# Scheduling priority for softmax chains, longer leads of fill, and an output pair whose operands load in two parts, in a two-layer hybrid decoder trunk

## The chip, the core and the metric

The kernel runs on one core of a Trainium2 chip. The metric is the device time of one execution in microseconds (us), the median over several runs. The core has a matrix engine (TensorE, "PE" in the profile, with its weight loads as "PEld"), three elementwise engines (VectorE "DVE", ScalarE "ACT", GpSimd "POOL") and SyncE ("SP"), which here issues nearly all DMAs. Each engine works through its own instructions in the order of the program.

## The reference

Two layers over a sequence of 1024 tokens with 1024 features, float32. Each layer adds the mixer's output and then a cross-attention over 256 memory tokens; a last norm follows.

```
for l in range(2):
    h = rms_norm(x, norm_mix_w[l])
    proj = h @ w_in                       # one projection for all three groups
    ya = sliding_window_attention(rope(q_a), rope(k_a), v_a, sinks) * silu(g_a)   # 8 heads, 2 kv heads, window 128
    yb = forgetting_attention(q_b, k_b, v_b, log_sigmoid(f_b + b)) * silu(g_b)    # 8 heads ("FoX"), causal, with decay
    yc = rms_norm((ssd(conv(xbc), dt, a) + d_skip * xs) * silu(z))                # state-space scan, chunks of 128
    x = x + concat(ya, yb, yc) @ w_out
    hq, mem_n = rms_norm(x, norm_xq_w[l]), rms_norm(mem, norm_mem_w[l])
    x = x + softmax((hq @ wq) @ (mem_n @ wk).T / 16) @ (mem_n @ wv) @ wo          # 4 heads of 256
return rms_norm(x, final_norm_w)
```

Both attentions normalise their scores with a softmax.

## The kernel before

Each float32 operand of a matmul is split into a high part and a remainder (`hi` on ScalarE, `lo` on VectorE or GpSimd), and each product is three matmuls (`mm3`, L111 to L113): high x high, low x high, high x low. Weights are streamed from memory and split on the way (`wload`: tiles `wst`, `whi`, `wlo`).

The order of work has two authors. TensorE's order is the order in which the Python code emits its matmuls. That order is made by `weave(main, fill)`: `main` is a generator for a chain with waits in it (a softmax, a norm), `fill` one for independent matmuls (projections, output products). Both yield costs, which add up to an estimated clock, `self.clock`. When `main` yields a number, the fill is advanced by that number times `self.ratio`, through an account called `owed`; when `main` yields a tuple `(time,)`, the fill is advanced until the estimated clock reaches that time, and what it takes is subtracted from `owed`; when `main` yields a string, the fill is advanced until that name is in `self.ready`. A fill that yields `None` has nothing to give for now. A "lead" below is such a wait of a fixed length: `yield (self.clock + 5.0,)`.

The order on the other engines and the DMA queues is made by a planner when the program is built. It keeps a priority for every instruction, the order of emission, and takes the first one that it thinks is ready; inside `tc.high_priority(n)` an instruction counts as if it had been emitted n places earlier.

The stages of one layer, with the lines that matter here:

- `tokmaj`: token-major projections (values, gates of the scan). In the second layer the norm of the second half of the sequence runs as `main` against the value projections of the first half.
- `mixer`: `fox_attend`, then `swa_attend`, then `ssd_scan` as `main`; as `fill` the projections of q, k and gates, the convolution and the output products. A FoX row (`fox_scores`) is scores on TensorE, maximum on VectorE (L604), negation (L605), exponential on ScalarE (L607), reciprocal (L608), normalisation on GpSimd (L609). Two rows are turned by `fox_turn` (transposes at L630, split at L77 and L85) and multiplied with the values at L667. A sliding-window unit (`swa_scores`, `swa_turn`) does the same for two heads at L779 to L791, with transposes at L802 and products at L834; the add at L542 collects the result and frees its PSUM buffer. `at[...]` says from when on a row may be turned. The rotary embedding of the sliding-window queries (`roped`, L720 and L721), gates (`gate`, L509 and L510) and weight splits use the same engines.
- `outproj`: the output product. For the first half of the sequence and the attention groups its first two tiles run as a pair, over the eight operand tiles in the order (4, 5, 6, 7, 0, 1, 2, 3); the last one is computed late and awaited by name (`y30`). The others are reloaded from memory into space of the normed activations (`load_ys`: a DMA, a cast on ScalarE, a subtraction on VectorE or GpSimd). The pair needs both accumulators (`acc`, two buffers), which the gate before it frees through L509 and L510.
- `tail`: the rest of the output product (`out_c`), the cross-attention and its output (`finish`). A norm (`norm_half`) begins with a lead; then `rstd` sums squares over partitions with small matmuls (L221), `spread` computes the inverse root and puts it on a diagonal (L232 to L242), waits through a second lead, and spreads it over all partitions with two matmuls (L251); then every tile is scaled (`normed`, L270) and split.

Of the kernel before, what the change touches and what calls it, by code (L numbers as in the profile page):

```python
# [12 lines left out]
ALU = mybir.AluOpType  # L13
# [30 lines left out]
class Net:  # L44
    def __init__(self, ctx, tc, a, out):
        self.ctx, self.tc, self.nc, self.a, self.out = ctx, tc, tc.nc, a, out
        self.n = 0
        self.pq = None
        self.alt_w = True
        self.ready, self.ratio, self.clock = set(), 1.0, 0.0  # L50
        self.alt = 0
        self.nb, self.ntp = 3, 2

    def psum(self):
        return self.tc.tile_pool(name=self.nm("pq"), bufs=1, reuse_waits="tile", space=PSUM)
# [172 lines left out]
    def spread(self, pool, ps, nch, rr):  # L228
        nc = self.nc
        with self.tc.high_priority(100):  # L230
            ms = self.tile(pool, [P, 4], F32, "nms", 2)
            nc.vector.tensor_scalar(out=ms[:, :nch], in0=ps[:, :nch], scalar1=EPS, scalar2=None, op0=ALU.add)  # L232
            rs = self.tile(pool, [P, 4], F32, "nrs", 2)
            nc.gpsimd.tensor_tensor(out=rs[:, :nch], in0=ms[:, :nch], in1=self.mhalf[:, :nch], op=ALU.pow)

            rp = self.tile(pool, [P, 2, 4], F32R, "nrp", 2)
            nc.vector.tensor_copy(rp[:, 0, :nch], rs[:, :nch])
            self.lo(rp[:, 1, :nch], rs[:, :nch], rp[:, 0, :nch])
            dg = self.tile(pool, [P, 2, 4, P], F32R, "ndg", 1)
            B3 = [P, nch, P]  # L240
            for i in range(2):
                nc.vector.tensor_tensor(  # L242
                    out=dg[:, i, :nch], in0=self.ident[:, None, :].to_broadcast(B3),
                    in1=f(rp[:, i, :nch, None]).to_broadcast(B3), op=ALU.mult,
                )
        self.rs = rs
        yield (self.clock + 5.0,)
        n = nch * P
        pb = self.tp()
        for i in range(2):  # L250
            nc.tensor.matmul(  # L251
                pb[:, :n], self.ones, dg[:, i, :nch].rearrange("p c d -> p (c d)"), start=i == 0, stop=i == 1
            )
        yield 0.43
        nc.scalar.copy(rr, pb[:, :n])
        return rr
# [16 lines left out]
        self.lo(lo, t[:, :n], hi, eng=nc.gpsimd if self.alt else nc.vector)  # L273

    def norm_half(self, pool, xs, accs, w, half):
        yield (self.clock + 3.0,)
        rr = yield from self.rstd(pool, accs, HALF)
        c = slice(half * HALF, (half + 1) * HALF)
        for k in range(KT):
            self.normed(pool, xs[k], w[:, k : k + 1], rr, HALF, self.hhi[:, k, c], self.hlo[:, k, c])  # L280
# [305 lines left out]
    def fox_scores(self, pool, t, e, i):  # L586
        nc = self.nc
        mm = nc.tensor.matmul
        Q1, Q2, K1, K2, _ = self.state["fox", t]
        n = (i + 1) * P  # L590
        S = self.big()
        q = slice(i * P, (i + 1) * P)
        cost = 0.0
        for b in range(0, n, HALF):
            w = min(HALF, max(256, n - b))
            diag = i * P < b + HALF
            k = slice(b, b + w)
            mm(S[:, k], Q1[e][:, q], K1[e][:, k], start=True, stop=False)  # L598
            mm(S[:, k], Q2[e][0:68, q], K2[e][0:68, k], start=False, stop=not diag)  # L599
            if diag:  # L600
                mm(S[:, q], self.identb, self.nmaskb, start=False, stop=True)  # L601
            cost += 2 * w / 2400 + 0.05 * diag
        sm = self.tile(pool, [P, 4], F32, "sm", 4)
        nc.vector.tensor_reduce(out=sm[:, 0:1], in_=S[:, :n], axis=AX.X, op=ALU.max)  # L604
        nc.vector.tensor_scalar(out=sm[:, 1:2], in0=sm[:, 0:1], scalar1=-1.0, scalar2=None, op0=ALU.mult)  # L605
        Pt = self.tile(pool, [P, T], F32, "Pt", 4)
        nc.scalar.activation(Pt[:, :n], S[:, :n], AF.Exp, bias=sm[:, 1:2], scale=1.0, accum_out=sm[:, 2:3])  # L607
        nc.vector.reciprocal(sm[:, 3:4], sm[:, 2:3])  # L608
        nc.gpsimd.tensor_scalar(  # L609
            out=Pt[:, :n], in0=Pt[:, :n], scalar1=sm[:, 3:4], scalar2=1.0, op0=ALU.mult, op1=ALU.mult  # L610
        )
        return Pt, cost


    def fox_turn(self, pool, Ps, kb, last):
# [9 lines left out]
        for d in range(2):  # L625
            for s in range(2):
# [1 line left out]
                    continue  # L628
                o = (2 * (1 - d) + s) * P
                nc.tensor.transpose(pt[:, o : o + P], Ps[s][:, (kb + d) * P : (kb + d + 1) * P], self.ident)  # L630
        self.hi(ph[:, c0:], pt[:, c0:])
        self.lo(pl[:, c0:], pt[:, c0:], ph[:, c0:])
        return ph, pl

    def fox_attend(self, l, pool):
# [5 lines left out]
        def scores(r):  # L641
            if r < len(rows):
                t, e, i = rows[r]
                if e == i == 0:
                    yield f"fox{t}"
                probs[r], cost = self.fox_scores(pool, t, e, i)
                yield cost
                at[r] = self.clock + 2.5 + 0.45 * (i + 1)

        at = {}  # L650
        yield from scores(0)
# [109 lines left out]
    def swa_scores(self, pool, t, i):  # L761
# [12 lines left out]
        for e in range(2):  # L774
            o = S[:, e * 256 : (e + 1) * 256]
            mm(o, Q1[e][:, q], K1[:, k0 : k0 + 256], start=True, stop=False)
            mm(o, Q2[e][:, q], K1[:, k0 : k0 + 256], start=False, stop=True)
        for e in range(2):
            nc.vector.tensor_tensor_reduce(  # L779
                out=Pt[:, e, :256], in0=S[:, e * 256 : (e + 1) * 256], in1=self.band[:, min(i, 1), :], scale=1.0,  # L780
                scalar=-3e38, op0=ALU.add, op1=ALU.max, accum_out=mx[:, 0, e : e + 1],
            )

        nc.vector.scalar_tensor_tensor(mx[:, 1], mx[:, 0], -1.0, self.nsk[:, h0 : h0 + 2], ALU.mult, ALU.min)
        for e in range(2):
            nc.scalar.activation(
                Pt[:, e, :257], Pt[:, e, :257], AF.Exp, bias=mx[:, 1, e : e + 1], scale=1.0, accum_out=mx[:, 2, e : e + 1]
            )
        nc.vector.reciprocal(mx[:, 3], mx[:, 2])
        o = Pt[:, :, :256]  # L790
        nc.gpsimd.tensor_tensor(out=o, in0=o, in1=mx[:, 3, :, None].to_broadcast([P, 2, 256]), op=ALU.mult)  # L791
        return Pt

    def swa_turn(self, pool, Pt):
# [73 lines left out]
    def mixer(self, l):  # L868
# [16 lines left out]
        def fill():  # L885
# [16 lines left out]
            for t in range(4):  # L902
# [4 lines left out]
                yield from self.noted(f"swag{t}", self.gate(l, t, T_GA + t, (0, 1) if t < 3 else (1, 0)))  # L907

            ys = self.early_ys
            self.load_ys(ys, order[:-1], 0)  # L910
            yield from self.noted(
                "ab0", self.outproj(self.fp, ("th", 3), l, 0, 0, ys, order, xin, pair=True, last="y30")
            )
            while "ab" not in self.ready:
                yield None
# [368 lines left out]
                put(values, pc, c, ps)  # L1284


    def outproj(self, pool, tag, l, half, s, ys, order, xin, after=None, pair=False, last=None):
        a = self.a
        c = slice(half * HALF, (half + 1) * HALF)
        for ms in ((0, 1), 2, 3, 4, 5, 6, 7) if pair else range(KT):  # L1290
            ms = ms if pair and ms == (0, 1) else (ms,)
            xt, ws, ps = {}, {}, {}
            for m in ms:
# [2 lines left out]
                ws[m] = self.wload(a["w_out"][l, m, s])  # L1296
                ps[m] = self.acc()
            for i, k in enumerate(order):
                while last and i == KT - 1 and last not in self.ready:
                    yield None  # L1300
                for m in ms:
# [25 lines left out]
    def tail(self, l, fp):  # L1327
# [9 lines left out]
        with self.pool("ma", 2) as ma:  # L1337
# [125 lines left out]
            self.weave(attend(1), finish(0, range(KT)))  # L1463
            self.ratio = 0.0
            if not last:
                self.weave(self.norm_half(pool, *self.sums[0], wn, 0), finish(1, range(KT)))
                return tl, (), self.norm_half(pool, *self.sums[1], wn, 1)
            self.weave(close(0, slice(0, HALF)), finish(1, range(KT - 1)))

# [153 lines left out]
```

## Time and profile before

| | |
|---|---|
| median of 3 runs | 2539.09 us (2537.62 to 2541.44) |
| the profiled execution | 2551.32 us, span of its instructions 2549.3 us |
| mean granted TensorE clock in it | 0.984 |
| TensorE busy | 2466.7 us |
| VectorE, ScalarE, GpSimd busy | 1545.4, 1189.0, 1166.9 us |
| memory read, written | 238.72 MB, 86.81 MB |

The profile is of one execution. Its views: the page with busy times; a table of stretches of time, with the busy time of each engine and the clock granted to TensorE (1.00 is full speed); the waits (which operation of an engine stood idle for which other one: total, times, longest); and the timeline, instruction by instruction (start, length, engine, line, operation, output<-inputs, and in brackets the idle time before it and what ended it). In the timeline a matmul's start-to-start distance tells more than its length, since matmuls overlap.

### The profile page before, as it was taken

How to read it: one execution, taken by the hardware profiler on the slowest of the kernel's cores; microseconds unless marked ns; L12 is line 12 of the kernel's file. 1: busy time of each engine (PE TensorE's matmuls, PEld its weight loads, DVE VectorE, ACT ScalarE, POOL GpSimd, SP SyncE). 2: the span in 40 equal slices, each digit the busy share in tenths (PEclk: the TensorE clock that was granted, in tenths of full speed). 3: DMA queues.
4: the chain of work that ended last, by engine and by line, in shares of the span. 5: the costliest groups of instructions: out<-in, count | busy, mean ns of one | idle time of the engine just before them, and what ended most of it. 6: DMA issues, size and time to landing. Idle time of an engine off the chain costs nothing.

```text
span 2549.3 us, 39348 instructions
## 1 busy us (share of the span) xinstructions
PE 2466.7 (97%) x13900; PEld 2081.7 (82%) x13900; DVE 1545.4 (61%) x2716; ACT 1189.0 (47%) x2455; POOL 1166.9 (46%) x1193
## 2 busy tenths in 40 slices
PE   8799999999999999999999999999999999999997
PEld 7799988888788777888879988888877877787886
DVE  6923166666778688654464226666668868764355
ACT  5532155545556455434443225455546645543442
POOL 5732144435566487432252124444446657732233
PEclk9999999999999999999999999999999999999999
DMA  7774132222222766553464223222223376554333
GB/s 235 217 237 111 65 98 70 66 88 86 81 87 90 246 221 195 162 169 116 128 195 120 78 68 92 70 79 84 89 71 90 115 256 209 170 185 151 119 93 132
DMA packets 230360, 333.37 MB, mean 131 GB/s; under 512 B 24370, under 2 KB 107442, under 8 KB 230148
## 3 DMA queue, kind: packets, MB, share of 16 engines
q1 hardware_dynamic: 228292, 328.76, 41.4%
q8 instruction: 110, 1.80, 0.3%
q10 hardware_dynamic: 1872, 2.10, 0.2%
q14 instruction: 86, 0.70, 0.1%
HBM read 238.72 MB, written 86.81 MB: 128 GB/s over the span
## 4 chain that ended last, share of the span: by engine, by line
PE 78%; DVE 7%; DMA 5%; issue 3%; ACT 3%; POOL 3%; SPq 1%; DVEq 0%; POOLq 0%; ACTq 0%
PE acc L111 16%; PE acc L112 15%; PE acc L113 15%; PE tp L667 3%; PE tp L630 2%; PE acc L372 2%; PE big L372 2%; PE acc L374 2%; PE big L374 2%; PE acc L373 2%; PE big L373 2%; SPq L72 1%; PE big L598 1%; PE big L599 1%; PE s L1128 1%
## 5 line engine op out<-in xcount | busy, mean ns | idle before, releaser
L111 PE MATMUL acc<-hhi,whi 128*128 128x512 f32 (+1 forms) x1960 | 796.8, 407 | 6.8 <-DVE th L510 5.4
L113 PE MATMUL acc<-hlo,whi 128*128 128x512 f32 (+1 forms) x1960 | 772.0, 394 | 0.0
L112 PE MATMUL acc<-hhi,wlo 128*128 128x512 f32 (+1 forms) x1960 | 771.6, 394 | 0.0
L85 POOL TENSOR_TENSOR wlo<-wst,whi 128x512 fp32r<-128x512 f32 x279 | 377.5, 1353 | 337.5 <-ACT whi L77 280.7
L113 PEld LDWEIGHTS acc<-hlo,whi 128*128 128x128 f32 x1960 | 372.0, 190 | 82.2
L111 PEld LDWEIGHTS acc<-hhi,whi 128*128 128x128 f32 x1960 | 374.2, 191 | 67.3 <-DVE th L510 5.8
L112 PEld LDWEIGHTS acc<-hhi,wlo 128*128 128x128 f32 x1960 | 373.8, 191 | 57.7
L77 ACT CAST whi<-wst 128x512 fp32r<-128x512 f32 x420 | 259.5, 618 | 302.8 <-PE acc L113 206.0
L77 ACT CAST ph<-tp 128x512 fp32r<-128x512 f32 (+1 forms) x256 | 142.5, 556 | 168.8 <-PE tp L630 118.0
L85 DVE TENSOR_TENSOR pl<-tp,ph 128x512 fp32r<-128x512 f32 (+1 forms) x256 | 167.0, 652 | 78.3 <-ACT ph L77 76.3
L85 DVE TENSOR_TENSOR wlo<-wst,whi 128x512 fp32r<-128x512 f32 x141 | 128.4, 910 | 118.0 <-ACT whi L77 117.2
L609 POOL TENSOR_SCALAR Pt<-Pt,sm 128x128 f32<-128x128 f32 (+7 forms) x128 | 105.8, 827 | 182.6 <-DVE sm L608 180.0
L1015 DVE SCALAR_TENSOR_TENSOR ac<-u,cw,ac 128x512 f32<-128x512 f32 x144 | 129.4, 899 | 34.0 <-POOL ac L1010 32.6
L85 POOL TENSOR_TENSOR tml<-tms,tmh 128x684 fp32r<-128x684 f32 (+3 forms) x40 | 67.4, 1703 | 132.7 <-ACT tmh L77 126.8
L607 ACT ACTIVATE Pt<-big,sm 128x128 f32<-128x128 f32 (+7 forms) x128 | 95.2, 743 | 69.8 <-DVE sm L605 62.3
L604 DVE TENSOR_REDUCE sm<-big 128x1 f32<-128x128 f32 (+7 forms) x128 | 96.1, 751 | 23.0 <-PE big L601 21.7
L372 PE MATMUL acc<-tmh,hhi 128*128 128x342 f32 (+3 forms) x320 | 102.1, 319 | 0.0
L372 PE MATMUL big<-tmh,hhi 128*128 128x342 f32 (+3 forms) x320 | 101.9, 318 | 0.0
L374 PE MATMUL acc<-tmh,hlo 128*128 128x342 f32 (+3 forms) x320 | 101.4, 317 | 0.0
L373 PE MATMUL big<-tml,hhi 128*128 128x342 f32 (+3 forms) x320 | 101.4, 317 | 0.0
L374 PE MATMUL big<-tmh,hlo 128*128 128x342 f32 (+3 forms) x320 | 101.4, 317 | 0.0
L373 PE MATMUL acc<-tml,hhi 128*128 128x342 f32 (+3 forms) x320 | 101.4, 317 | 0.0
(339 smaller groups left out, 5151.1 us busy)
## 6 DMA issues: line engine op xcount, KB each, us to landing
wst<-in_w_fm_dram SPq DMA_DIRECT2D x132, 256.0 KB
wst<-in_w_out_dram SPq DMA_DIRECT2D x128, 256.0 KB
wst<-in_w_mq_dram SPq DMA_DIRECT2D x64, 256.0 KB
wst<-in_w_mo_dram SPq DMA_DIRECT2D x64, 256.0 KB
xt<-x_st SPq DMA_DIRECT2D x48, 256.0 KB
v_st<-vt SPq DMA_DIRECT2D x32, 320.0 KB
vs<-v_st SPq DMA_DIRECT2D x20, 512.0 KB
xs_st<-tr SPq DMA_DIRECT2D x40, 256.0 KB
```

The source lines that it names most:

```text
L77: self.nc.scalar.copy(out, in_)
L85: (eng or self.nc.vector).tensor_tensor(out=out, in0=in_, in1=f(hi), op=ALU.subtract)
L111: mm(ps, ahi, bhi, start=first, stop=False)
L112: mm(ps, alo, bhi, start=False, stop=False)
L113: mm(ps, ahi, blo, start=False, stop=last)
L372: mm(ps[:, :n], self.hhi[:, k, cs], hi[:, k, :n], start=k == 0, stop=False)
L373: mm(ps[:, :n], self.hhi[:, k, cs], lo[:, k, :n], start=False, stop=False)
L374: mm(ps[:, :n], self.hlo[:, k, cs], hi[:, k, :n], start=False, stop=k == KT - 1)
L604: nc.vector.tensor_reduce(out=sm[:, 0:1], in_=S[:, :n], axis=AX.X, op=ALU.max)
L607: nc.scalar.activation(Pt[:, :n], S[:, :n], AF.Exp, bias=sm[:, 1:2], scale=1.0, accum_out=sm[:, 2:3])
L609: nc.gpsimd.tensor_scalar(out=Pt[:, :n], in0=Pt[:, :n], scalar1=sm[:, 3:4], scalar2=1.0, op0=ALU.mult, op1=ALU.mult)
L1015: nc.vector.scalar_tensor_tensor(ac, u[:, 5 + j : 5 + j + HALF], w[:, t, j : j + 1], ac, ALU.mult, ALU.add)
```

## The change

Five edits, all in the order of work; none adds or removes an instruction.

- The softmax of `fox_scores` and of `swa_scores`, and the split in `fox_turn`, are emitted inside `tc.high_priority(60)`. The split in `swa_turn` and the chain in `spread` had `high_priority(100)` before and keep it.
- The lead in front of every `norm_half` becomes 6.0 in place of 3.0.
- The lead in `spread` becomes a field, `self.slag`, which is 5.0 as before, but 9.0 in one place: the norm of the first half for the next layer, at the end of the first layer's `tail`.
- In `fox_attend`, `at` is 3.2 in place of 2.5 after the row's scores (plus 0.45 for each block of keys).
- `load_ys` before the output pair loads six operand tiles in place of seven; the seventh, tile 2, is loaded from within `outproj`, after the products of the first operand tile were emitted (`behind`).

```diff
+        self.slag = 5.0
...
-        yield (self.clock + 5.0,)
+        yield (self.clock + self.slag,)
...
     def norm_half(self, pool, xs, accs, w, half):
-        yield (self.clock + 3.0,)
+        yield (self.clock + 6.0,)
...
(fox_scores; the same around L779 to L791 in swa_scores and the split in fox_turn)
+        with self.tc.high_priority(60):
+            nc.vector.tensor_reduce(out=sm[:, 0:1], in_=S[:, :n], axis=AX.X, op=ALU.max)
...
+            nc.gpsimd.tensor_scalar(
...
(fox_attend)
-                at[r] = self.clock + 2.5 + 0.45 * (i + 1)
+                at[r] = self.clock + 3.2 + 0.45 * (i + 1)
...
-            self.load_ys(ys, order[:-1], 0)
+            self.load_ys(ys, order[:-2], 0)
             yield from self.noted(
-                "ab0", self.outproj(self.fp, ("th", 3), l, 0, 0, ys, order, xin, pair=True, last="y30")
+                "ab0",
+                self.outproj(
+                    self.fp, ("th", 3), l, 0, 0, ys, order, xin, pair=True, last="y30",
+                    behind=lambda: self.load_ys(ys, order[-2:-1], 0),
+                ),
             )
...
(outproj)
             for i, k in enumerate(order):
+                if behind and i == 1:
+                    behind()
+                    behind = None
...
(tail)
             if not last:
+                self.slag = 9.0
                 self.weave(self.norm_half(pool, *self.sums[0], wn, 0), finish(1, range(KT)))
+                self.slag = 5.0
```

More of the change, by code (lines that the diff above doesn't have):

```diff
@@ L603, in fox_scores @@
         sm = self.tile(pool, [P, 4], F32, "sm", 4)
-        nc.vector.tensor_reduce(out=sm[:, 0:1], in_=S[:, :n], axis=AX.X, op=ALU.max)
-        nc.vector.tensor_scalar(out=sm[:, 1:2], in0=sm[:, 0:1], scalar1=-1.0, scalar2=None, op0=ALU.mult)
         Pt = self.tile(pool, [P, T], F32, "Pt", 4)
[L607 to L611, printed above, removed]
+        with self.tc.high_priority(60):
+            nc.vector.tensor_reduce(out=sm[:, 0:1], in_=S[:, :n], axis=AX.X, op=ALU.max)
+            nc.vector.tensor_scalar(out=sm[:, 1:2], in0=sm[:, 0:1], scalar1=-1.0, scalar2=None, op0=ALU.mult)
+            nc.scalar.activation(Pt[:, :n], S[:, :n], AF.Exp, bias=sm[:, 1:2], scale=1.0, accum_out=sm[:, 2:3])
+            nc.vector.reciprocal(sm[:, 3:4], sm[:, 2:3])
+            nc.gpsimd.tensor_scalar(
+                out=Pt[:, :n], in0=Pt[:, :n], scalar1=sm[:, 3:4], scalar2=1.0, op0=ALU.mult, op1=ALU.mult
+            )
         return Pt, cost
@@ L630, in fox_turn @@
                 nc.tensor.transpose(pt[:, o : o + P], Ps[s][:, (kb + d) * P : (kb + d + 1) * P], self.ident)
-        self.hi(ph[:, c0:], pt[:, c0:])
-        self.lo(pl[:, c0:], pt[:, c0:], ph[:, c0:])
+        with self.tc.high_priority(60):
+            self.hi(ph[:, c0:], pt[:, c0:])
+            self.lo(pl[:, c0:], pt[:, c0:], ph[:, c0:])
         return ph, pl
@@ L777, in swa_scores @@
             mm(o, Q2[e][:, q], K1[:, k0 : k0 + 256], start=False, stop=True)
[L778 to L791, printed above, removed]
+        with self.tc.high_priority(60):
+            for e in range(2):
+                nc.vector.tensor_tensor_reduce(
+                    out=Pt[:, e, :256], in0=S[:, e * 256 : (e + 1) * 256], in1=self.band[:, min(i, 1), :], scale=1.0,
+                    scalar=-3e38, op0=ALU.add, op1=ALU.max, accum_out=mx[:, 0, e : e + 1],
+                )
+            nc.vector.scalar_tensor_tensor(mx[:, 1], mx[:, 0], -1.0, self.nsk[:, h0 : h0 + 2], ALU.mult, ALU.min)
+            for e in range(2):
+                nc.scalar.activation(
+                    Pt[:, e, :257], Pt[:, e, :257], AF.Exp, bias=mx[:, 1, e : e + 1], scale=1.0,
+                    accum_out=mx[:, 2, e : e + 1],
+                )
+            nc.vector.reciprocal(mx[:, 3], mx[:, 2])
+            o = Pt[:, :, :256]
+            nc.gpsimd.tensor_tensor(out=o, in0=o, in1=mx[:, 3, :, None].to_broadcast([P, 2, 256]), op=ALU.mult)
         return Pt
@@ L1284, in memkv, with outproj @@
                 put(values, pc, c, ps)
-    def outproj(self, pool, tag, l, half, s, ys, order, xin, after=None, pair=False, last=None):
+    def outproj(self, pool, tag, l, half, s, ys, order, xin, after=None, pair=False, last=None, behind=None):
         a = self.a
```

## The prediction

> **What bounds the kernel now.** I read the page's busy times first, then the table by stages, then TensorE's waits, then the stretches of half clock.
>
> ```profile
> span 2549.3 us, 39348 instructions
> PE 2466.7 (97%) x13900; PEld 2081.7 (82%) x13900; DVE 1545.4 (61%) x2716; ACT 1189.0 (47%) x2455; POOL 1166.9 (46%) x1193
> ```
>
> TensorE (PE) is busy 97% of the span and no other engine above 61%. The change removes no matmul, so all it can win is time in which PE stands or runs slowly. The table by stages (length, then busy us of PE, weight load, DVE, ACT, POOL, then the granted clock) says where that is:
>
> ```profile
> 150.00:650.00 500.00, 498.05 (x2829) 436.97 (x2828) 257.85 (x481) 209.72 (x433) 184.06 (x234) 1.00 0.31 94
> 720.00:860.00 140.00, 131.87 (x737) 112.01 (x736) 108.99 (x300) 89.76 (x242) 86.04 (x100) 0.98 0.36 111
> ...
> 1345.00:1850.00 505.00, 502.89 (x2854) 441.00 (x2853) 270.95 (x498) 214.48 (x441) 185.54 (x235) 1.00 0.28 84
> ```
>
> From the token-major projections through most of the FoX attention PE loses 1.95 us in 500 and 2.11 us in 505; in the sliding-window (SWA) stage, where DVE is busy 78%, it loses 8.1 in 140. Who ends PE's waits (total, times, longest):
>
> ```profile
> PE tp L251 <- DVE ndg L242: 9.1, 5, 4.0
> PE tp L221 <- DVE nac L265: 6.8, 3, 2.7
> ...
> PE acc L111 <- DVE th L510: 5.4, 2, 2.8
> PE tp L802 <- POOL Pt L791: 5.1, 7, 1.1
> PE tp L667 <- DVE pl L85: 4.8, 4, 2.4
> PE tp L630 <- POOL Pt L609: 4.4, 2, 2.2
> PE tp L802 <- DVE ys L542: 4.0, 6, 1.0
> ```
>
> The first two lines are the norms, the third an output pair that waits for its accumulator, the next three the softmax and its split, the last a released PSUM buffer. Each wait has a second price. The stretches of granted clock 0.50 after the start and before the end (columns as above):
>
> ```profile
> 848.56:851.97 3.41, 3.41 (x14) 3.02 (x13) 2.78 (x6) 2.37 (x7) 0.93 (x2) 0.50 0.90 312
> 1101.15:1107.98 6.83, 6.83 (x19) 5.49 (x19) 2.48 (x7) 1.10 (x2) 1.66 (x2) 0.50 0.22 73
> 1299.12:1305.95 6.83, 5.68 (x14) 4.31 (x14) 4.61 (x4) 3.23 (x7) 5.90 (x5) 0.50 0.59 177
> ...
> 2046.64:2053.47 6.83, 6.05 (x18) 5.07 (x19) 5.37 (x13) 3.82 (x11) 3.14 (x3) 0.50 0.69 230
> 2302.64:2309.47 6.83, 6.83 (x19) 5.55 (x20) 2.55 (x7) 1.10 (x2) 1.60 (x2) 0.50 0.24 73
> sum 47.78, PE 45.45 PEld 36.85 DVE 26.98 ACT 15.82 POOL 24.94; mean PE 4.54 PEld 3.69 DVE 2.70 ACT 1.58 POOL 2.49
> ```
>
> Ten stretches, 47.78 us: four of 6.83, and six of 3.41 (848 and five around the end of FoX and the first SWA rows of both layers). Each begins within a few us of a wait named above.
>
> **The change, part by part.**
>
> *Norm lead 3 to 6.* After the last output tile PE gets this much of fill before the sums at L221:
>
> ```profile
> 1098.31 0.39 PE L112 MATMUL acc<-hhi,wlo 128*128 128x512 f32 x1
> 1098.54 0.39 PE L113 MATMUL acc<-hlo,whi 128*128 128x512 f32 x1
> 1100.64 1.38 PE L221 MATMUL tp<-onecol,nac 128*128 128x1 f32 x8 [1.71 <-DVE nac L265]
> ...
> 1104.15 0.63 PE L113 MATMUL acc<-hlo,whi 128*128 128x512 f32 x1
> 1104.58 0.63 PE L111 MATMUL acc<-hhi,whi 128*128 128x512 f32 x1
> 2302.16 1.40 PE L221 MATMUL tp<-onecol,nac 128*128 128x1 f32 x8 [2.70 <-DVE nac L265]
> ```
>
> A step of fill is three matmuls at 0.23 us each (1098.31 to 1098.54), 0.69 us for 0.64 of the kernel's clock. Lead 3 is five steps, lead 6 ten: 3.4 us more matmuls in front of L221, more than either wait. So 1.71 + 2.70 = 4.4 us go. Behind the wait the matmuls start 0.43 us apart (1104.15 to 1104.58) in place of 0.23; a slow stretch so costs 47% of its length, 3.2 us for 6.83 and 1.6 for 3.41. Two long ones: 6.4. Together 10.8; bounds 0 and 10.8, and I take 10.8, since both waits are shorter than the added fill; 0 would need the square-sum itself to come later by as much. What covers it is the q projection (one tile is 24 matmuls, 5.5 us), whose weights are two tiles ahead. The norm's results come 3.4 us later, with most of that projection's eight tiles still to run. The third wait in the L221 row (6.8 - 4.4 = 2.4) is in the start, where PE waits for weights as well; 0 to 2.4, I take 0.
>
> The same lead also delays the norm that runs under the value projections of layer 1, where the last normed tile is only just in time:
>
> ```profile
> 1369.83 0.69 DVE L85 TENSOR_TENSOR hlo<-ntm,hhi 128x512 fp32r<-128x512 f32 x1
> ...
> 1372.06 0.32 PE L373 MATMUL big<-tml,hhi 128*128 128x344 f32 x1
> 1372.22 0.32 PE L374 MATMUL big<-tmh,hlo 128*128 128x344 f32 x1
> ```
>
> Row tile 7 is complete at 1370.5 and read at 1372.2: 1.7 us spare. The lead here is 7 steps of 0.43, and 14 after; a step is three matmuls 0.16 us apart (the last two rows), so the norm comes 7 x 0.48 = 3.4 us later and PE would wait 1.7. With a long slow stretch it would be 4.9, and 0 if DVE catches up. I take -1.7, since no other work of PE is queued there to cover it.
>
> *Row lead 5 to 9 in one place* (the norm of layer 1's first half):
>
> ```profile
> 1289.41 0.95 PE L221 MATMUL tp<-onecol,nac 128*128 128x1 f32 x8
> 1298.07 2.36 DVE L242 TENSOR_TENSOR ndg<-ident,nrp 128x512 fp32r<-128x512 f32 x2
> 1298.80 0.54 PE L251 MATMUL tp<-ndg,ones 128*128 128x512 f32 x1 [2.85 <-DVE ndg L242]
> 1300.48 0.79 PE L251 MATMUL tp<-ndg,ones 128*128 128x512 f32 x1 [1.15 <-DVE ndg L242]
> ```
>
> Nine of clock are 15 steps of 0.69 from about 1290.2: L251 would come at 1300.5, just when the second ndg is done (1298.07 + 2.36). So 2.85 + 1.15 and a 3.2 slow stretch, 7.2 at most; 0 if POOL, which held this chain, is as much later. I take 6.5. The other waits in the L251 row (9.1 - 4.0) lie at the start and in the last norms, which keep 5.
>
> *One tile of the output pair loaded later.* In the FIFO of ACT the cast of this tile stands ahead of the tanh that frees the accumulator:
>
> ```profile
> 845.82 0.62 ACT L77 CAST hhi<-hlo 128x512 fp32r<-128x512 f32 x1 [2.17 <-DMA hlo<-y_st]
> 846.34 0.59 ACT L509 ACTIVATE th<-acc 128x512 f32<-128x512 f32 x1
> ...
> 847.70 0.50 PE L111 MATMUL acc<-hhi,whi 128*128 128x512 f32 x1 [2.54 <-DVE th L510]
> ...
> 2047.42 0.79 PE L111 MATMUL acc<-hhi,whi 128*128 128x512 f32 x1 [2.85 <-DVE th L510]
> ```
>
> Moved behind the first products, one DMA, one cast and one subtraction leave that place. The tanh then starts as soon as its matmuls are done, and 2.54 + 2.85 go, with slow stretches of 1.6 and 3.2: 10.2 at most. What may be late next is the tile itself: on SP it queues behind the pair's inputs, and it is used in the seventh of eight steps, 6 x 2 x 0.69 = 8 us after the pair's start; a DMA that lands 3 us late in both layers gives back 6. So 10.2 to 4.2 less a slow stretch each; I take 7.
>
> *Softmax priority.* The planner's order on DVE, ACT and POOL puts these operations ahead of up to 60 earlier ones. POOL's FIFO at the last FoX rows shows what for:
>
> ```profile
> 695.40 1.09 POOL L609 TENSOR_SCALAR Pt<-Pt,sm 128x896 f32<-128x896 f32 x1
> 696.45 1.73 POOL L85 TENSOR_TENSOR wlo<-wst,whi 128x512 fp32r<-128x512 f32 x1
> ...
> 698.52 1.20 POOL L131 TENSOR_SCALAR q<-q 64x512 fp32r<-64x512 f32 x2
> 699.82 1.12 POOL L609 TENSOR_SCALAR Pt<-Pt,sm 128x1024 f32<-128x1024 f32 x1
> ```
>
> Between the two normalisations lie 3.2 us of weight split and copies, for rows that PE then waits 2.2 for. The rows that can go are L802 on POOL (5.1), L667 (4.8) and L630 (4.4), 14.3, and five slow stretches of 1.6: 22.3. Priority helps only where the planner thinks both ready at once, so the bounds are 0 and 22.3, and I take half, 11: 9.5 of the 14.3 lie on POOL, whose FIFO is shown here, and not all of that will tie. What is overtaken (weight splits, rope, evictions) has slack by FoX's table; in SWA the add that frees a PSUM buffer (L542, 4.0 in six waits) is not raised and may come later. Bounds 0 and -8 (three times the row), I take -4.
>
> *FoX lead 2.5 to 3.2.* More fill before each turn, paid back by the weave's account in later steps. It can win at most the 1.95 + 2.11 of the table: I take 2.5. The lead costs no matmul.
>
> **Sum**: 10.8 - 1.7 + 6.5 + 7 + 11 - 4 + 2.5 = 32.1 us. The profiled execution took 2551.32 (span 2549.3 and 2.0 around it), so 2519.2; the median is 2539.09, 0.9952 of it: 2507.
>
> [...] The rows have half clock after waits of 1.71 to 2.85 us. [...]
>
> **Rivals.**
> 1. Priority does nothing: DVE and POOL keep their order because the planner sees no tie, so the waits of SWA stay. Then 32.1 - 11 + 4 = 25.1 goes: 2526.2 by the profile, 2514 by the median. For it: FoX has hardly a wait to show; against it: the POOL rows.
> 2. The slow stretches stay, set off by what is left of the waits. Of the sum 6.4 (norms), 2.9 (row lead, 6.5 of 7.2 x 3.2), 3.3 (split, 7 of 10.2 x 4.8) and 4 (priority, half of 8) are clock, 16.6 together. That leaves 15.5: 2524. For it: a wait of only 1.71 was enough for 6.83 us.
> 3. Slower: in SWA the raised softmax delays the L542 add and the turn's split. There are 64 SWA units in both layers, and DVE is busy 78%. Above (36 + 5) / 64 = 0.64 us per unit the kernel is slower by over 0.2%; 36 being the sum without its own -4. At 0.8, a fifth above the mean wait of that row (4.0 / 6 = 0.67), it is 51 us: 2539 + 15 = 2554. Against it: only six of 64 units wait there now.
> 4. Fill runs out before the end of the scan: 32 turns x 0.7 of longer FoX lead is 22 us a layer taken early. Where it isn't given back PE stands at the scan's end; with 16 us a layer the gain is gone: 2539. Against it: what a wait takes is subtracted from what the next steps get.
>
> **How the numbers follow.** Chances: forecast 0.54, rival 1 0.20, rival 2 0.08, rival 3 0.09, rival 4 0.09. 0.2% (5 us) is about what can be told from no change. Faster: forecast, rivals 1 and 2, less 0.01 = 0.81; within: rival 4; slower: rival 3 and that 0.01 = 0.10. With every term at its best (10.8 + 2.4 + 7.2 + 10.2 + 22.3 + 4.1) the gain is 57 us, 2483; that needs all of them, so the range begins at 2490 and leaves out some 0.05 below. Above it takes in rivals 1 and 2 and the near half of rival 4, and ends at 2537; rival 3 and the rest of 4 (0.14) stay out. The forecast's own range is 2493 to 2521.
>
> **What would show it.** The L221 rows at 1100 and 2302 without a wait, no half clock behind them; no wait at L251 near 1300; no ACT cast on a y DMA ahead of L509; POOL's L609 back to back; L609 and L791 rows shorter in PE's waits. Wrong if L542, L510 or the seventh pair step appear there with over 15 us, if PE waits for hlo near 1370 by over 3, or if PE stands before the tail.

## The result, and the profile after

The changed kernel takes 2557.64 us (median of 6 runs, 2550.51 to 2563.8), the kernel before 2541.24 (6 runs beside it, 2537.62 to 2543.49): ratio 1.0071, 95% interval 1.0056 to 1.0085. It is slower by 0.7%, where 1.3% faster was forecast.

The profiled execution took 2563.8 us. From its page, the span and the busy times (lines of the changed kernel stand 1 to 12 lower: L222, L252 and L243 are L221, L251 and L242 of before, L632 and L670 are L630 and L667):

```profile
span 2562.1 us, 39362 instructions
PE 2464.5 (96%) x13900; PEld 2079.2 (81%) x13900; DVE 1539.9 (60%) x2716; ACT 1191.0 (46%) x2455; POOL 1169.6 (46%) x1193
```

The span is 12.8 us longer and PE is 2.2 us less busy: what came is idle time. The table by stages says where. First before (length, then busy us of PE, weight load, DVE, ACT, POOL, the granted clock): FoX of both layers, and the stretch from the end of the scan to the cross-attention of both.

```profile
319.30:714.30 395.00, 389.07 (x2090) 322.75 (x2089) 255.69 (x468) 200.75 (x411) 180.83 (x250) 1.00 0.27 81
1514.90:1912.40 397.50, 390.77 (x2091) 324.02 (x2090) 255.65 (x468) 200.82 (x411) 180.82 (x250) 0.99 0.26 80
...
1021.00:1145.40 124.40, 122.69 (x592) 100.17 (x592) 75.76 (x100) 54.19 (x92) 46.03 (x37) 0.97 0.53 167
2221.50:2347.00 125.50, 122.80 (x592) 100.24 (x592) 75.76 (x100) 54.10 (x92) 46.06 (x37) 0.97 0.53 166
```

Then the same four stretches after:

```profile
324.30:731.30 407.00, 394.21 (x2099) 326.23 (x2099) 261.05 (x471) 202.95 (x415) 186.95 (x252) 0.99 0.26 79
1525.00:1934.60 409.60, 395.95 (x2099) 327.35 (x2098) 261.07 (x471) 202.91 (x415) 186.47 (x252) 0.99 0.26 78
...
1037.00:1156.30 119.30, 119.30 (x593) 97.88 (x593) 72.64 (x100) 54.88 (x92) 46.08 (x37) 1.00 0.57 175
2240.40:2359.70 119.30, 119.30 (x592) 97.89 (x592) 72.67 (x100) 54.89 (x92) 46.23 (x37) 1.00 0.56 175
```

The norms did as forecast: 5.1 and 6.2 us gone, PE busy without a gap, full clock. But FoX is 12.0 and 12.1 us longer. PE stands 12.8 and 13.7 us in it (length less busy), 5.9 and 6.7 before; nine matmuls more run there. The stretch from the first token-major product to FoX grew by 6.3 us (175.48 to 181.78).

TensorE's waits after (total, times, longest):

```profile
PE tp L632 <- DVE sm L608: 13.9, 14, 2.6
...
PE tp L670 <- DVE sm L608: 7.3, 7, 2.4
PE tp L252 <- DVE ndg L243: 7.0, 4, 4.0
...
PE acc L112 <- DVE th L511: 4.4, 2, 2.4
PE tp L807 <- DVE ys L543: 3.8, 5, 1.0
PE big L374 <- POOL tml L86: 3.7, 3, 1.6
```

The waits for the norm's sums are gone from the list. New at its head is FoX's turn (L632), 13.9 us in 14 waits for VectorE; in the list before, the turn waited 4.4 us for POOL and 1.7 for VectorE. The sliding-window products (L839, L834 before) wait 7.5 us for the split of their turn, in place of 1.1.

The places that the prediction named, in TensorE's timeline after:

```profile
1118.18 0.95 PE L222 MATMUL tp<-onecol,nac 128*128 128x1 f32 x8
...
1315.90 0.50 PE L252 MATMUL tp<-ndg,ones 128*128 128x512 f32 x1 [0.98 <-DVE ndg L243]
1317.57 0.79 PE L252 MATMUL tp<-ndg,ones 128*128 128x512 f32 x1 [1.17 <-DVE ndg L243]
...
2321.59 0.95 PE L222 MATMUL tp<-onecol,nac 128*128 128x1 f32 x8
...
1381.42 0.42 PE L373 MATMUL big<-tmh,hhi 128*128 128x344 f32 x1 [0.70 <-ACT hhi L78]
...
865.45 0.50 PE L112 MATMUL acc<-hhi,whi 128*128 128x512 f32 x1 [2.04 <-DVE th L511]
...
2068.20 0.55 PE L112 MATMUL acc<-hhi,whi 128*128 128x512 f32 x1 [2.37 <-DVE th L511]
```

The sums at L222 no longer wait. The row sums at L252 still wait 2.15 of 4.00 us. The pair's first product still waits for the tanh, 2.04 and 2.37 in place of 2.54 and 2.85.

### The profile page after: what moved, and what is told of

Read it like the earlier page. It is cut to its first block, busy times and chain, and to the rows that moved or that the text cites. A ratio compares the mean times of both kernels' runs of the same rounds, so it can differ in the third digit from the quotient of the medians.

```text
span 2562.1 us, 39362 instructions
## 1 busy us (share of the span) xinstructions
PE 2464.5 (96%) x13900; PEld 2079.2 (81%) x13900; DVE 1539.9 (60%) x2716; ACT 1191.0 (46%) x2455; POOL 1169.6 (46%) x1193
## 4 chain that ended last, share of the span: by engine, by line
PE 75%; DVE 10%; DMA 5%; ACT 3%; issue 3%; POOL 3%; SPq 1%; DVEq 0%; POOLq 0%; ACTq 0%
PE acc L112 15%; PE acc L113 15%; PE acc L114 15%; PE tp L670 2%; PE acc L373 2%; PE acc L375 2%; PE acc L374 2%; PE tp L632 2%; PE big L375 2%; PE big L374 2%; PE big L373 2%; DVE ac L1024 1%; PE s L1137 1%; DVE pl L86 1%; DMA xs_st<-tr 1%
## 5 line engine op out<-in xcount | busy, mean ns | idle before, releaser
L112 PE MATMUL acc<-hhi,whi 128*128 128x512 f32 (+1 forms) x1960 | 788.5, 402 | 6.2 <-DVE th L511 4.4
L86 DVE TENSOR_TENSOR wlo<-wst,whi 128x512 fp32r<-128x512 f32 x141 | 121.8, 864 | 99.4 <-ACT whi L78 99.0
L1024 DVE SCALAR_TENSOR_TENSOR ac<-u,cw,ac 128x512 f32<-128x512 f32 x144 | 130.6, 907 | 37.3 <-POOL ac L1019 35.7
L632 PE MATMUL tp<-ident,Pt 128*128 128x128 f32 x576 | 90.6, 275 | 17.9 <-DVE sm L608 13.9
L632 PEld LDWEIGHTS tp<-ident,Pt 128*128 128x128 f32 x576 | 71.2, 140 | 44.3 <-issue 15.7
L374 PE MATMUL big<-tml,hhi 128*128 128x342 f32 (+3 forms) x320 | 102.2, 319 | 3.7 <-POOL tml L86 3.7
```

What stands on the lines that cost most here:

```text
L86: (eng or self.nc.vector).tensor_tensor(out=out, in0=in_, in1=f(hi), op=ALU.subtract)
L112: mm(ps, ahi, bhi, start=first, stop=False)
L374: mm(ps[:, :n], self.hhi[:, k, cs], lo[:, k, :n], start=False, stop=False)
L1024: nc.vector.scalar_tensor_tensor(ac, u[:, 5 + j : 5 + j + HALF], w[:, t, j : j + 1], ac, ALU.mult, ALU.add)
```

## The experiments

Sixteen kernels. "FoX" is the time from the first mask product to the first sliding-window score, layer 0 and layer 1, in the profiled execution; its waits are the sum of PE's waits there. Each ratio is against runs of the kernel before made beside that run, whose medians lie between 2538.24 and 2541.24 us; so medians of different runs are compared to a few us only.

### Which edit it is

**a: all edits but the priority.** Edit, at the three places:

```diff
-        with self.tc.high_priority(60):
+        if True:
```

> The changed kernel without its three raised priorities; leads and split stay. Theory P (the raised softmax makes VectorE's order worse in FoX: long maxima stand ahead of the split that PE's turn waits for): the FoX stage goes from 407.0 and 409.7 us (two layers, changed kernel) back to 395 to 398, and the time falls below the kernel before, to 2526 to 2532. Theory F (the longer FoX lead shifts PE's order so that turns meet the split too early, priority is harmless): FoX stays at 405 to 410, time about 2555.

Measured 2558.28 us, ratio 1.0078 [1.0062, 1.0095]; FoX 405.8 and 406.6, waits 11.6 and 12.3. As slow as with the priority, which so takes no part in the loss: theory F's forecast, and not theory P's.

**b: all edits, but the FoX lead back at 2.5.**

```diff
-                at[r] = self.clock + 3.2 + 0.45 * (i + 1)
+                at[r] = self.clock + 2.5 + 0.45 * (i + 1)
```

> The changed kernel with the FoX lead back at 2.5; priorities, norm leads and split stay. Theory P: FoX stays at 405 to 410, time 2550 to 2558. Theory F: FoX 395 to 398, time 2526 to 2532.

Measured 2533.76, ratio 0.9987 [0.9974, 1.0000]; FoX 394.8 and 395.1, waits 5.5 and 6.1. With the lead back at 2.5 the whole loss is gone, much as theory F said.

**c: the leads of the norms and rows, and the split** (a and b together).

> Norm leads (6 and 9) and the split pair alone, no priority, FoX lead 2.5. Both theories: FoX 395 to 398; the stretch from the scan's end to the cross-attention stays at 119.3 in both layers (124.5 and 125.5 before); time 2526 to 2532. If neither P nor F holds and the longer norm leads themselves cost FoX, FoX stays above 405.

Measured 2532.44, ratio 0.9977 [0.9967, 0.9986]; FoX 394.8 and 395.1, and 119.3 us from the scan's end to the cross-attention in both layers, as forecast; the time is just above its 2526 to 2532. Its instructions stand in the same order as in b on every engine: with the lead at 2.5, raising the softmax by 60 places changed nothing that the planner did. With 3.2 (the changed kernel against a) it moved one add (L543) behind a maximum (L783) in each layer's sliding-window stage, on VectorE, and nothing on the other engines. The 1.3 us between b and c are therefore what two measurements of one program differ by here.

**d: the leads of norms and rows alone** (c without the split).

```diff
-            self.load_ys(ys, order[:-2], 0)
+            self.load_ys(ys, order[:-1], 0)
...
-                    behind=lambda: self.load_ys(ys, order[-2:-1], 0),
```

> Norm leads alone (6 and 9): no priority, FoX lead 2.5, no split. If the split wins the 7 us of the prediction, this is 7 above the kernel with norms and split; if the accumulator's wait is left by the split (2.0 and 2.4 us in the changed kernel against 2.5 and 2.8), it is within 2 us of it. FoX 395 to 398 in either case.

Measured 2536.7, ratio 0.9992 [0.9980, 1.0005]. Against b and c, which are one program, the split so is worth 3 to 4 us (2536.7 less 2533.76 and 2532.44), with intervals that overlap at their ends: less than the 7 of the prediction, more than the 2 of the other case. The waits for the tanh say less: 2.25 and 2.45 us in d, 1.83 and 2.17 in c.

**e: the FoX lead alone, on the kernel before.** `2.5` becomes `3.2` in the line of b.

> The kernel before with the FoX lead at 3.2 and nothing else. If the lead alone makes the loss (theory F), the FoX stages are 405 to 410 us and the time is 20 to 28 above the kernel before, about 2562. If it needs the shifted norms as well, FoX is near 395 and the time within 5 of before.

Measured 2555.16, ratio 1.0061 [1.0047, 1.0075]; FoX 404.3 and 406.9, waits 11.4 and 12.8. One constant makes a loss without any of the other edits. It is smaller than expected, though: 15.4 us above the kernel before beside it (2539.79), where 20 to 28 were expected, and 25.8 where the other edits are in (a over c). In the profiles it is 18.8 us in FoX here and 22.5 there.

### Why a longer lead costs time

**Two theories.** The wait `(at,)` takes its fill out of the account `owed`. With 3.2 there is more fill before a unit's first turn, and less before a later one. "Spacing": that later turn then comes too close. Rival: the lead itself does the harm.

**f: lead 3.2 with more fill ahead of one turn** (c otherwise).

```diff
-                t_ = self.clock + TURN
+                t_ = self.clock + (2.9 if kb == 2 else TURN)
```

> Norm leads and split, FoX lead 3.2, and the wait between the second and the third turn of a row pair 2.9 in place of 2.2, which puts one fill step more there. Theory F1 (the longer first lead is paid back between the later turns, which come too early for VectorE's split): the waits at the third turn (7.0 us of 11.6 in a layer) go, FoX is 395 to 400 and the time 2533 to 2545. Theory F2 (any order of the fill in which VectorE has convolution or maxima ahead of the split costs the same, wherever the turn stands): waits of 9 us or more in a FoX stage stay, FoX is 403 or more, time 2550 to 2560.

Measured 2546.65, ratio 1.0037 [1.0021, 1.0053]; waits in FoX 9.4 and 9.7. It moved 60 matmuls from the sliding-window stage into FoX (412.8 and 413.2, the other 148.3 and 148.2), so the two must be read together: 561.0 and 561.4 us against 555.8 and 555.6 in c and 567.3 and 568.4 in a. One step more ahead of one turn removes about half. The wait at that turn went as the first theory said: PE's waits at L632 for VectorE fell from 8.8 us to 1.7 in layer 0. But the products at L670 now wait 5.8 us in place of 2.7 and the first turns 2.0 in place of 0.2, so the other theory's 9 us stayed, and the time lies between the two forecasts.

**g: a shorter lead, 1.9** (c otherwise).

> Norm leads and split, FoX lead 1.9 in place of 2.5. Theory F1: later turns get at least the spacing they had, so that only the first turn of a pair can come too early: FoX 394 to 399, time 2531 to 2541. Theory F2 (2.5 happens to fall well, and any other lead falls worse): FoX 400 or more in both layers, time over 2543.

Measured 2523.95, ratio 0.9935 [0.9922, 0.9949]; FoX 391.2 and 390.5, waits 4.0 and 3.1. Faster than both kernels, and than either theory forecast: the lead was too long before the change already.

**f2: a shorter smallest distance of turns with the lead at 2.5** (c otherwise).

```diff
-                t_ = self.clock + TURN
+                t_ = self.clock + 1.6
```

> Edit: kernel c (leads of the norms and the split, no priority, FoX lead 2.5), with the smallest distance between two FoX turns 1.6 of clock in place of 2.2. Theory 'spacing': the longer lead hurts because what it takes is charged to the fill steps between the turns after it, so that these turns come closer than VectorE can split the turned rows. Then a smaller distance hurts in the same way with the lead unchanged: FoX 394.8 and 395.1 become 400 to 410 us a layer, TensorE's waits in FoX 5.5 and 6.1 become 9 to 15, the time 2532 becomes 2545 to 2562. Rival 'lead': the lead itself is the harm (a row that is turned later frees its buffers later), whatever lies between the turns: then FoX stays within 2 us of c, and the time within 4 us of 2532, or falls, since rows are turned sooner.

Measured 2540.36, ratio 0.9998 [0.9982, 1.0013]. The median rose by 8 us over c's (5 by the ratios), but not where spacing wanted it: FoX took 396.4 and 394.5, within 2 us of c; waits 8.1 and 6.5. That doesn't refute spacing, since the edit thins another place than the longer lead does: ahead of the second turn, while the account gives the fill back ahead of the third (the table below). Where this kernel's other microseconds went was not followed up.

**i, j: still shorter leads, 1.2 and 0.5** (c otherwise).

> Edit: kernel c with a FoX lead of 1.2 (2.5 in c; 1.9 gave 2523.95 us, 3.2 some 2557). Theory 'spacing': the account then pays back more between the turns, but the first turn now comes sooner after its scores, and the softmax (maximum, exponential, normalisation, some 4 us by their durations) is no longer covered. I expect the best lead near 1.9: 2520 to 2530 us, with TensorE's waits for POOL at the turn (under 1 us a layer with 1.9) rising by 1 to 4 a layer while those for VectorE stay at 3 to 4. Rival 'the shorter the better': 2515 to 2519, FoX 384 to 388 us a layer.

> Edit: kernel c with a FoX lead of 0.5. As for 1.2, farther out: theory 'spacing' with the softmax uncovered expects 2525 to 2545 us, the first turn after the scores waiting for POOL's normalisation. If the minimum distance between turns already sets the first turn (the lead no longer binds), it equals the run with 1.2 within 3 us. Rival 'the shorter the better': below 2519.

Measured 2533.32, ratio 0.9975 [0.9959, 0.9991], FoX 395.6 and 393.2; and 2538.97, ratio 0.9995 [0.9981, 1.0010], FoX 397.3 and 398.3. So the curve has a minimum: 0.5, 1.2, 1.9, 2.5, 3.2 give 2539, 2533, 2524, 2532, 2558 (ratios 0.9995, 0.9975, 0.9935, 0.9977, 1.0078). "The shorter the better" is refuted; 0.5 came out as expected, 1.2 missed its 2520 to 2530, and 7.1 of its 9.4 us over 1.9 lie in FoX.

**Where the fill goes.** TensorE's order shows it. Counted in steps of three matmuls, mean per turn, in layer 0's FoX (layer 1 has the same numbers); "first" takes in all fill since the last turn of the unit before. The last column is PE's wait at the third turn of layer 0:

| run | lead | first | second | third | fourth | wait at the third, us |
|---|---|---|---|---|---|---|
| j | 0.5 | 7.39 | 2.42 | 3.75 | 3.00 | 0 |
| i | 1.2 | 7.60 | 2.33 | 3.44 | 3.00 | 0 |
| g | 1.9 | 8.01 | 2.33 | 2.62 | 3.00 | 0.4 |
| c | 2.5 | 8.39 | 2.33 | 1.94 | 3.00 | 0.9 |
| a | 3.2 | 8.67 | 2.33 | 1.56 | 3.00 | 8.8 |
| f | 3.2, one step more | 8.79 | 2.33 | 2.56 | 3.00 | 1.7 |
| f2 | 2.5, turns closer | 8.70 | 1.33 | 2.94 | 2.38 | 0.9 |

The lead moves fill from ahead of the third turn to ahead of the first, and hardly anywhere else. With 3.2 the third turn waits 8.8 of the 11.6 us, and with its step back (run f) only 1.7. So spacing holds, at the third turn. TensorE's waits in layer 0's FoX (total, times, longest); the largest line with lead 0.5:

```profile
PE tp L632 <- POOL Pt L611: 3.5, 4, 1.1
```

Lead 1.9:

```profile
PE tp L670 <- DVE sm L608: 1.5, 2, 0.9
```

Lead 3.2 (run a):

```profile
PE tp L632 <- DVE sm L608: 7.0, 7, 2.6
```

The same line with the step back (run f):

```profile
PE tp L632 <- DVE sm L608: 1.7, 2, 1.3
```

With the lead at 0.5 the first turn waits for POOL's normalisation of the row, 3.5 us where 1.9 has 0.6; 4.5 us more are waits for VectorE. With 1.2 no turn waits in layer 0, but the products at L670 wait 6.2 us for VectorE. With 3.2 the third turn waits for VectorE.

**What VectorE does instead.** In a, the first long wait of a turn, in VectorE's timeline and then TensorE's:

```profile
347.99 3.32 DVE L1024 SCALAR_TENSOR_TENSOR ac<-u,cw,ac 128x512 f32<-128x512 f32 x3
351.34 0.69 DVE L86 TENSOR_TENSOR pl<-tp,ph 128x512 fp32r<-128x512 f32 x1
351.95 1.08 DVE L607 TENSOR_REDUCE sm<-big 128x1 f32<-128x896 f32 x1
...
353.61 1.22 DVE L607 TENSOR_REDUCE sm<-big 128x1 f32<-128x1024 f32 x1
354.74 1.16 DVE L1024 SCALAR_TENSOR_TENSOR ac<-u,cw,ac 128x512 f32<-128x512 f32 x1
355.82 0.68 DVE L86 TENSOR_TENSOR pl<-tp,ph 128x512 fp32r<-128x512 f32 x1
```

```profile
356.65 0.59 PE L632 MATMUL tp<-ident,Pt 128*128 128x128 f32 x3 [1.92 <-DVE sm L608]
```

And the same unit in c:

```profile
344.91 1.08 DVE L607 TENSOR_REDUCE sm<-big 128x1 f32<-128x896 f32 x1
345.91 1.24 DVE L1027 SCALAR_TENSOR_TENSOR th<-th,ac 128x512 f32<-128x512 f32 x1
347.07 0.14 DVE L608 TENSOR_SCALAR sm<-sm 128x1 f32<-128x1 f32 x1
347.13 0.68 DVE L86 TENSOR_TENSOR pl<-tp,ph 128x512 fp32r<-128x512 f32 x1
347.73 1.21 DVE L607 TENSOR_REDUCE sm<-big 128x1 f32<-128x1024 f32 x1
```

```profile
347.87 0.55 PE L632 MATMUL tp<-ident,Pt 128*128 128x128 f32 x3
```

TensorE has the same work between the second and the third turn in both. What differs is VectorE's order. In c the split `pl` of the second turn stands ahead of the 1024-wide maximum. In a it stands behind that maximum and behind a tap of the convolution (L1024), 2.38 us more, though ScalarE's cast before it was done at 353.71. The third turn (L632) needs the PSUM buffer which that split reads; the profile names the negation L608, the small operation next to it (356.50). In c the turn follows that split as closely (it ends at 347.81), and the negation had ended at 347.21.

**l, m, n: no convolution taps on VectorE,** at leads 3.2, 2.5 and 1.9 (on a, c and g). These kernels leave three of the convolution's four taps out, and TensorE's work stays as it is:

```diff
-            for j in range(1, 4):
-                nc.vector.scalar_tensor_tensor(ac, u[:, 5 + j : 5 + j + HALF], w[:, t, j : j + 1], ac, ALU.mult, ALU.add)
```

> Edit: kernel a (all edits but the priority, FoX lead 3.2) without the convolution's three tap multiplies on VectorE, which leaves that part of the convolution out; they are 60.2 of VectorE's 261 us in layer 0's FoX. Theory 'VectorE backlog': the third turn waits because the split before it stands behind these multiplies. Then TensorE's waits in FoX fall from 11.6 and 12.3 to 3 to 6 a layer, FoX from 405.8 and 406.6 to 394 to 398, and the time from 2558 to 2530 to 2540. Rival 'the distribution of fill': TensorE has too little work between the turns whatever VectorE does besides; the waits stay at 9 or more, FoX above 402, the time above 2548.

> Edit: kernel c (the same with FoX lead 2.5) without the three tap multiplies. The control of the run before. Theory 'VectorE backlog': FoX 391 to 394 us a layer (394.8 and 395.1 with the taps), within 4 us of lead 3.2 without them. Rival: 390 to 395, and 8 or more below lead 3.2 without them.

> Edit: the kernel with FoX lead 1.9 without the three tap multiplies. Theory 'VectorE backlog': nothing is left to win from the lead, FoX equal to lead 2.5 without taps within 2 us (390 to 392 a layer). Rival: 2 to 4 us a layer below lead 2.5 without taps, as with the taps (391.2 and 390.5 against 394.8 and 395.1).

Measured: lead 3.2, 2543.47, ratio 1.0012 [0.9999, 1.0025], FoX 400.2 and 398.8, waits 8.9 and 9.0. Lead 2.5, 2533.75, ratio 0.9973 [0.9961, 0.9986], FoX 394.2 and 395.7, waits 6.4 and 6.5. Lead 1.9, 2523.76, ratio 0.9936 [0.9918, 0.9954], FoX 390.5 and 389.5.

With the taps, 3.2 costs 11.0 and 11.5 us a layer over 2.5; without them 6.0 and 3.1. The taps are 60 us of VectorE's work in a FoX stage, and at 2.5 and 1.9 taking them away moves the time by 1.3 us at most. So some 60% of the lead's price (13.4 of 22.5 us) is the backlog of the convolution on VectorE, and neither forecast was met: 394 to 398 was wanted for all of it, 402 for none. Run m lies just above the 391 to 394 that the backlog theory gave it. At the third turn the wait fell from 8.8 to 5.1 us:

```profile
PE tp L632 <- DVE sm L608: 5.1, 4, 2.6
```

What remains is partly other work in the same queue. Run l, at its longest wait (VectorE, then TensorE):

```profile
402.44 1.23 DVE L607 TENSOR_REDUCE sm<-big 128x1 f32<-128x1024 f32 x1
403.69 0.69 DVE L86 TENSOR_TENSOR k<-stg,k 64x512 fp32r<-64x512 f32 x1
404.41 0.69 DVE L86 TENSOR_TENSOR pl<-tp,ph 128x512 fp32r<-128x512 f32 x1
```

```profile
405.25 0.87 PE L632 MATMUL tp<-ident,Pt 128*128 128x128 f32 x3 [2.56 <-DVE sm L608]
```

Here a split of the next keys stands there in place of the tap. Another part is the nine matmuls more in FoX, 9 x 0.23 = 2.1 us (0.23 from start to start, as at 1098.31 and 1098.54 in the kernel before), which the sliding-window stage has less, so that the kernel doesn't pay for them. And between 2.5 and 1.9 lie 3.7 and 6.2 us a layer without the taps too, as n's rival said: that part of the curve isn't the convolution.

**Left open.** Why the planner puts `pl` behind the maximum and the tap with the one lead and ahead of them with the other was not measured. It orders by its own estimate of when things are ready, and `pl` is emitted earlier than the 1024-wide maximum with either lead, so it has the higher priority already; raising it by 60 places left the waits of L632 at 13.9 us with the priority and without (run a).

### A version that is faster

**h: the short lead of 3 kept for three norms** (c otherwise): the two at the start and the one under layer 1's value projections.

```diff
-    def norm_half(self, pool, xs, accs, w, half):
-        yield (self.clock + 6.0,)
+    def norm_half(self, pool, xs, accs, w, half, lead=6.0):
+        yield (self.clock + lead,)
```

> Norm leads and split, but the two norms at the start and the one under layer 1's value projections keep lead 3. If their longer lead costs what the stages show (the wait of POOL's split in the first token-major products, 3.5 us and a slow stretch; 1.4 us in layer 1's), the time is 4 to 8 below the kernel with norms and split, 2525 to 2529. If the start only trades one wait for another, it is within 2 of it, 2531 to 2535.

Measured 2533.4, ratio 0.9973 [0.9962, 0.9983], against 2532.44 of c: no difference by the time. The profiles differ, though. From the start to FoX took 317.7 us in the mean of the five profiled kernels with the short lead there (315.8 to 319.8), and 321.6 in the thirteen with the long one (318.0 to 324.8). The token-major stage is 5.6 us longer with the long lead, and what stands ahead of it 1.7 shorter. So the long lead costs some 4 us there by the profiles; the medians of h and c don't show it, and h's forecast of 4 to 8 us was missed.

**k, o: lead 1.9 with h's short leads, row lead 11 and 9.**

```diff
-                self.slag = 9.0
+                self.slag = 11.0
```

> Edit: the run with FoX lead 1.9 (2523.95 us), with the short lead of 3 kept for the two norms at the start and for the one under the value projections of layer 1, and the row lead 11 in place of 9. The two kept leads were worth nothing on kernel c (2533.4 against 2532.4); the row lead can take the 0.98 + 1.17 us that still stood at L252 and the stretch of 3.41 us at half clock, 3.8 us at most. Expected 2519 to 2525; tail of layer 0 from 71.5 to 68 us. Rival: the start and the token-major stage lose what they won with lead 6, 2524 to 2530.

> Edit: the last version (FoX lead 1.9, short lead kept for three norms) with row lead 9 in place of 11. The tail of layer 0 took 76.6 us there with 7.7 us of waits, and 71.5 with row lead 9 and the long tokmaj lead. If the lead of 11 ran the tail out of fill, it goes back to 71 to 72 and the time to 2520 to 2523; if it was the short norm lead, the tail stays at 75 to 77 and the time at 2525.

Measured: k 2525.01, ratio 0.9946 [0.9926, 0.9966], tail of layer 0 76.6 us; o 2521.19, ratio 0.9922 [0.9907, 0.9938], tail 73.8. A row lead of 11 is no gain: k's tail was forecast at 68. For o the time was met and the tail was not (71 to 72, or 75 to 77). Run o is the fastest, 0.8% below the kernel before; its FoX in the table by stages:

```profile
317.10:707.40 390.30, 387.11 (x2088) 320.70 (x2087) 258.94 (x467) 199.84 (x411) 180.56 (x249) 1.00 0.26 81
1502.10:1892.40 390.30, 387.20 (x2087) 320.73 (x2086) 259.02 (x467) 199.69 (x411) 180.54 (x249) 1.00 0.26 81
```

PE stands 3.2 and 3.1 us there, a quarter of what it does after the change, and the clock is full.

## Why the prediction was wrong, term by term

**The step that failed: the FoX lead, priced at +2.5, cost 24** (2557.64 - 2533.76; 25.8 from c to a; 15.4 on the kernel before, run e). The prediction said: "It can win at most the 1.95 + 2.11 of the table", and "The lead costs no matmul." The first took its bound from stretches that end at 650 and 1850, ahead of FoX's end: the whole stage stood 5.9 and 6.7 us, and run g took 3.8 and 7.0 off it. The second is true. Neither is a lower bound. I bounded this term from above alone, since the account pays the fill back, and did not ask what the paid-back fill had been covering: the time that VectorE needs ahead of the third turn, in a queue that it shares with the convolution. Without it that turn waits 8.8 us a layer. The table of stages that I used to show that FoX had little to win (2 us of idle time in 500) said nothing of what it had to lose. None of the rivals named this. Rival 4 came nearest (fill taken early), but looked for the price at the end of the scan; there PE is busy 119.30 of 119.30 us.

**Priority, +11: 0.** Rival 1 was right on this term. The condition was in the prediction ("only where the planner thinks both ready at once"), and half of the bound was taken all the same, because POOL's queue was seen out of order. That a queue holds other work between two urgent operations doesn't show that the planner saw a tie.

**Norm lead in the tails, +10.8: 11.3** (124.40 and 125.50 to 119.30 twice). Both the waits and their stretches of half clock went. That there were two stretches to win was partly luck of the profiled execution: in run e, which keeps the lead of 3, the same wait in layer 0 (1.68 us) has none behind it, the two stages take 121.2 and 124.6 us, and the lead would be worth 7.2. So rival 2 is refuted here: waits of 1.71 and 2.70 us had half clock behind them (0.50, from 1101.15 and 2302.64), and without the waits it was gone (1.00 in both stages after).

**The same lead at the start, 0 to +2.4, taken as 0: about -4,** by the eighteen profiles above. I named the wait that it might take away and not the one that it brings (the last row of the waits after, `L374` for POOL, 3.7 us in three waits, none of which stood in the list before).

**Under the value projections, -1.7: -1.4** (176.9 to 178.2 us), 0.70 of it the wait shown; the rest was not placed.

**Row lead, +6.5: not to be told from 0.** The wait fell by 1.85 us, as POOL and VectorE, which held the chain, came later too (the "0" of the bounds): from the sums to the second ndg it was 10.1 us before and 12.9 after. The tail of layer 0 took 73.6 before and 71.4 after, but 69.9 in run e with the old lead, and 71.2 to 74.9 in the other kernels with the new one. In ten of the fifteen kernels with the lead of 9 a new wait of 2.35 to 4.93 us stands soon behind L252; in the two with the old lead there is none over 0.7. Runs c and k (lead 11):

```profile
1306.38 0.47 PE L112 MATMUL acc<-hhi,whi 128*128 128x512 f32 x1 [3.15 <-ACT hhi L78]
```

```profile
1304.04 0.77 PE L112 MATMUL acc<-hhi,whi 128*128 128x512 f32 x1 [7.66 <-DVE xt L1438]
```

This looks like the error of the FoX lead once more: steps taken ahead of L252 are missing behind it, where a product waits for its operand or its accumulator. No run tests that.

**Split, +7: 3 to 4.** The cast that waits for a DMA did not leave ScalarE's way. ScalarE's timeline after:

```profile
863.56 0.62 ACT L78 CAST hhi<-hlo 128x512 fp32r<-128x512 f32 x1 [1.69 <-DMA hlo<-y_st]
864.09 0.59 ACT L510 ACTIVATE th<-acc 128x512 f32<-128x512 f32 x1
```

I took the order in which the code emits for the order on ScalarE. The planner makes that one, and it still put a cast ahead of the tanh; the wait for its DMA only fell from 2.17 to 1.69 us.

**New waits in the sliding-window stage, -4: 0 to -2.** PE's waits there went from 8.1 and 9.9 us to 10.9 and 10.2, and the stage's length from 161.1 and 163.9 to 160.9 and 161.3, with nine matmuls less. Rival 3 did not occur: the waits at the add (L543) are 3.8 us, 4.0 before. The turn's split, which it names too, is waited for longer (L839, 7.5 us in place of 1.1), but as long without the priority (7.5 in a), and 0.9 with the lead at 2.5 (c): this comes with the FoX lead.

With the FoX lead left at 2.5 (b and c, one program, ratios 0.9987 and 0.9977) the sum's other terms came to 3 to 6 us, of 29.6 forecast. By the terms above, 11 of the difference is the priority, 4 to 6 the row lead, 3 to 4 the split and 4 the start.

## What to carry to other kernels

A constant that only moves independent work has no free direction: price the side that loses the work, by asking which other engine's queue used that time and what else stands in it. A stage with hardly any idle time can win little and can still lose, so bound such a term below, not only above; then try the constant in both directions, since the better value here lay on the other side (1.9, where 2.5 stood and 3.2 was tried). And before a priority is priced, show one place where the planner had the choice.

## What was not expected of the hardware

Waits of 1.91 and 2.56 us at FoX's turn, ending at 358.12 and 413.15 us, had stretches of 3.41 us at a granted clock of 0.50 beside them in the changed kernel, beginning at 358.44 and at 413.05, so that the second began inside its wait. With lead 1.9 no wait in FoX is over 0.9 us (run g), and the clock is 1.00 in both layers (the rows of run o).

Nor did every such wait have one, as the prediction's "second price" assumes: the wait of 2.04 us that ends at 865.45 in the changed kernel had none, nor had 3.15 us in run c (1306.38). The traces of the kernel before and of the changed kernel show when it came. In each of them the stretches of half clock begin whole multiples of 3.413 us apart (358.44 and 413.05 are 16 such steps apart). Cut into windows on that grid, from 150 us behind the start to 60 us ahead of the end, the two executions have 1349 windows at full clock. In 16 of them PE stood 1.91 to 2.85 us, and the next window had half clock behind all 16; in four it stood 1.71 to 1.84 us, and three had it; in the other 1329 it stood 1.47 us at most, and none had it. Five such windows (columns as in the table by stages): one of the kernel before, ahead of the stretch at 1101.15; two of run e, around the same wait, which the grid cuts at 1103.70; and two of the changed kernel.

```profile
1097.74:1101.15 3.41, 1.70 (x11) 1.19 (x9) 1.99 (x2) 1.77 (x3) 1.27 (x1) 1.00 0.67 219
...
1100.29:1103.70 3.41, 2.06 (x10) 1.37 (x8) 2.09 (x3) 1.55 (x3) 1.27 (x1) 1.00 0.93 337
1103.70:1107.12 3.42, 3.09 (x18) 2.77 (x19) 1.75 (x6) 0.22 (x1) 1.01 (x1) 1.00 0.57 162
...
863.61:867.02 3.41, 1.57 (x9) 1.34 (x10) 2.31 (x6) 2.06 (x4) 2.52 (x2) 1.00 0.51 150
409.64:413.05 3.41, 0.95 (x6) 0.48 (x4) 3.32 (x6) 1.49 (x3) 2.01 (x5) 1.00 0.24 87
```

PE stands 1.71, 1.35, 0.33, 1.84 and 2.46 us in them; half clock follows the first and the last. So, in these traces, a slow stretch came behind every window with 1.91 us or more of idle time, and the wait of run e, which the grid cuts into 1.35 and 0.33 us, had none.
